# A conformer layer on one core: the convolution's normalization and activation transpose through the convolution's own PSUM banks, and the second sigmoid follows the last rounding

## The chip, the cores and the metric

The kernel runs on one core of one Trainium2 chip. The metric is the device time of one launch in microseconds, the median of several runs. An execution that the hardware profiler recorded gives the span, the rows and the granted TensorE clock quoted here.

## What is computed

One layer on x of 256 rows and 1024 columns, all in fp32:

```
x = x + 0.5 * swiglu(rms_norm(x, g1), w_gate, w_up, w_down)
proj = rms_norm(x, gm) @ w_in
conv_a, conv_b, q, k, v, gate_a, gate_b = split(proj)
u = causal_depthwise_conv(conv_a * sigmoid(conv_b))       # 31 taps
u = silu(layer_norm(u, gain, bias))
y_a = u @ w_conv_proj
y_b = attention(rms_norm(q), rms_norm(k), v) @ w_attn_proj    # 16 heads, causal
x = x + (sigmoid(gate_a) * y_a + sigmoid(gate_b) * y_b) @ w_out
x = x + 0.5 * swiglu(rms_norm(x, g2), w_gate2, w_up2, w_down2)
```

## The kernel before, in words

Every dense product goes through `gemm` (L137). A product of a column chunk of 512 is cut into pieces of two 128-row blocks of the weight; each piece is one transfer of 512 KB from SyncE (SP) into a ring of five `raw` buffers. ScalarE rounds the piece to the matmul type (`hi`, L100), VectorE or GpSimd subtracts (`lo`, L102), both in rings of five, and TensorE runs three matmuls of 512 columns for each block and each half t of the 256 rows (L165 to L167: hi times hi, hi times lo, lo times hi). A transposed activation is split in the same two parts. The results lie in PSUM: a ring `acc` of three banks (L66), a ring `cv` of two banks for the convolution (L69), and a ring `tr` of three banks for transposes and the attention (L72).

The stages follow each other: first feed-forward, input projection `w_in` (14 chunks, in the order of `W_IN`), attention projection `w_attn` (two chunks, `wb`), convolution projection `w_conv` (two chunks, `wa`), output projection `w_out`, second feed-forward. The attention (`score`, `flip`, `value`, L458 to L536) and the convolution are generators that are pumped between the pieces of the input projection and of the first chunk of the attention projection. The written order is only the start: a scheduler that simulates the engines puts the instructions of each engine in order when the program is built, and a ring's bank must have been read before its next user writes it. So which ring an instruction draws from changes where it lands.

What the change touches stands between the attention's end and the convolution projection:

- `conv` (L330) accumulates 31 taps in two `cv` banks on VectorE, and ScalarE copies them back into the tiles `uT` (L350). Four such pairs run one after the other.
- `conv_norm` (L352) transposes `uT` back to rows: for each half t two groups of four transposes (L359) into one PSUM bank each, a ScalarE copy into `ynat` (L364); then VectorE's statistics (L368, L370), `rsqrt_mean` (ScalarE scaling L185, GpSimd power L187), and VectorE's normalization of the half (L375).
- `conv_act` (L378) transposes `ynat` once more, four groups of four transposes (L385), each into one bank; ScalarE applies gain, bias and Silu into `z` (L392, two buffers) and rounds it (`u2h`, L398), VectorE subtracts (`u2l`, L399). `u2h` and `u2l` are what the convolution projection multiplies.
- `run` calls `sigmoid` (L699) on `gate_b` with `issue_after` the attention's last rounding (`oh`, L220), and on `gate_a` with `issue_after` what `conv_act` returns. Sigmoid, Silu and the attention's exponential need different activation tables, so each change of function has a row `ACT_TABLE_LOAD`. `gate_b` is multiplied with the attention projection (L714), `gate_a` with the convolution projection (L722).

Of the kernel before, what the change touches and what calls it, by code (L numbers as in the profile page):

```python
# [50 lines left out]
class Build:  # L51
# [300 lines left out]
    def conv_norm(self, yT, ynat):  # L352
        nc = self.nc
        for t in range(2):
            for c0 in range(0, KD, 4):
                ps = self.tr()
                for q in range(4):
                    c = c0 + q
                    nc.tensor.transpose(  # L359
                        ps[:, q * P : (q + 1) * P],  # L360
                        yT[c // 2][:, (c % 2) * S + t * P : (c % 2) * S + (t + 1) * P],
                        self.ident,
                    )
                nc.scalar.copy(ynat[:, t * D + c0 * P : t * D + (c0 + 4) * P], ps)  # L364
                yield 1
            st = self.tmp.tile([P, 2, 6], F32, tag="bst", name="bst", bufs=2)
            for c in range(2):
                nc.vector.bn_stats(st[:, c, :], ynat[:, t * D + c * CH : t * D + (c + 1) * CH])  # L368
            mv = self.tmp.tile([P, 2], F32, tag="mv", name="mv", bufs=2)
            nc.vector.bn_aggr(mv, st)  # L370
            r = self.rsqrt_mean(mv[:, 1:2], 1, 1)
            yield 1
            for c in range(2):
                y = ynat[:, t * D + c * CH : t * D + (c + 1) * CH]
                nc.vector.tensor_scalar(y, y, mv[:, 0:1], r, ALU.subtract, ALU.mult)  # L375
            yield 1

    def conv_act(self, ynat, hi, lo, after):  # L378
        nc = self.nc
        cst = self.cst  # L380
        for c in range(0, KD, 2):
            ps = self.tr()
            for q in range(2):
                for t in range(2):
                    nc.tensor.transpose(  # L385
                        ps[:, q * S + t * P : q * S + (t + 1) * P],
                        ynat[:, t * D + (c + q) * P : t * D + (c + q + 1) * P], self.ident,
                    )
            z = self.tmp.tile([P, CH], F32, tag="junk", name="z", bufs=2)
            with self.tc.issue_after(after.ins):  # L390
                for q in range(2):
                    last = nc.scalar.activation(  # L392
                        z[:, q * S : (q + 1) * S], ps[:, q * S : (q + 1) * S], AF.Silu,
                        bias=cst[:, C_LB + c + q : C_LB + c + q + 1],
                        scale=cst[:, C_LG + c + q : C_LG + c + q + 1],
                    )
            h = hi[:, c * S : (c + 2) * S]
            nc.scalar.copy(h, z)  # L398
            nc.vector.tensor_tensor(lo[:, c * S : (c + 2) * S], z, h.bitcast(F32), ALU.subtract)  # L399
        return last  # L400


    def head_norm(self, acc, rstd, c, dst, gain, rq=None):
# [437 lines left out]
```

## Time and profile before

| | |
|---|---|
| median of 3 runs | 647.08 us (646.92 to 647.13) |
| profiled execution | 647.48 us, span 645.6 us, mean granted TensorE clock 0.995 |
| TensorE busy | 634.2 us (98%), weight loads 516.8 us |
| VectorE, ScalarE, GpSimd busy | 369.9, 362.5, 164.9 us |
| DMA | 114.97 MB, mean 178 GB/s |

Times in rows are microseconds from the start of the span. A timeline row gives start, duration, engine, line, operation, what is written and read, how many, and in brackets the idle time of the engine before it and what ended it. Matmuls are pipelined, so the rows of neighbours overlap: the distance of two starts is what a matmul costs. The granted clock (PEclk) is a share of full speed; 1.00 is 2.4 GHz and 0.50 is 1.2 GHz.

### The profile page before, as it was taken

Reading aid. Unit: us, or ns where it says so; the run is one execution under the profiler, and the core shown is the slowest. Engines: PE = TensorE matmul, PEld = TensorE weight load, DVE = VectorE, ACT = ScalarE, POOL = GpSimd, SP = SyncE. Lnnn points to the kernel's source line nnn. Section 1 sums busy time; section 2 is a strip of 40 time slices with the busy share of each in tenths; the row PEclk is TensorE's granted clock in tenths of the full one; section 3 lists DMA queues with packets and bytes.
Section 4 is the critical chain, followed back from the end, with each engine's and each line's share of the span. In section 5 each row is a group of like instructions: output and inputs, shape, how many; then the busy total and the mean of one; then the engine's idle time right before and its main releaser. Section 6 shows DMA issues by size and latency. Waiting matters only on the chain.

```text
span 645.6 us, 8133 instructions
## 1 busy us (share of the span) xinstructions
PE 634.2 (98%) x2952; PEld 516.8 (80%) x2952; DVE 369.9 (57%) x625; ACT 362.5 (56%) x547; POOL 164.9 (26%) x83
## 2 busy tenths in 40 slices
PE   9999999999999999999999997899999999999997
PEld 7788888888888888777777785788888888888886
DVE  5655464554542699879313936485664546465541
ACT  6755354443545676987876667744655435444330
POOL 0100000000006999689866761000100000000000
PEclk9999999999999999999999999799999999999999
DMA  8966556567564555545654552264755656556630
GB/s 271 354 232 192 199 173 195 160 198 219 174 201 135 178 170 180 171 130 169 196 158 135 164 168 96 96 199 153 224 163 186 196 177 198 189 168 200 197 124 32
DMA packets 32855, 114.97 MB, mean 178 GB/s; under 512 B 3632, under 2 KB 4912, under 8 KB 32816
## 3 DMA queue, kind: packets, MB, share of 16 engines
q1 hardware_dynamic: 32816, 114.46, 55.9%
q8 instruction: 23, 0.38, 0.2%
q14 instruction: 16, 0.13, 0.1%
HBM read 113.40 MB, written 1.05 MB: 177 GB/s over the span
## 4 chain that ended last, share of the span: by engine, by line
PE 64%; DVE 2%; ACT 1%; issue 0%; DVEq 0%
PE acc L165 20%; PE acc L166 20%; PE acc L167 19%; PE tr L465 1%; PE tr L211 1%; PE tr L529 1%; PE tr L512 1%; DVE lo L102 1%; PE tr L438 1%; DVE bst L368 0%; ACT gate_b L703 0%; ACT z L392 0%; PE tr L655 0%; DVE gate_b L714 0%; ACT L703 0%
## 5 line engine op out<-in xcount | busy, mean ns | idle before, releaser
L100 ACT CAST hi<-raw 128x1024 fp32r<-128x1024 f32 (+1 forms) x216 | 223.1, 1035 | 220.3 <-PE acc L167 184.4
L102 DVE TENSOR_TENSOR lo<-raw,hi 128x1024 fp32r<-128x1024 f32 (+1 forms) x156 | 186.2, 1197 | 167.2 <-ACT hi L100 162.7
L102 POOL TENSOR_TENSOR lo<-raw,hi 128x1024 fp32r<-128x1024 f32 x60 | 143.7, 2420 | 200.3 <-ACT hi L100 200.2
L347 DVE SCALAR_TENSOR_TENSOR cv<-uT,cst,cv 128x255 f32<-128x255 f32 (+28 forms) x240 | 95.2, 465 | 8.4 <-ACT cv L343 8.2
L166 PE MATMUL acc<-lo,h1h 128*128 128x512 f32 x224 | 88.3, 394 | 0.0
L165 PE MATMUL acc<-hi,h1h 128*128 128x512 f32 x224 | 88.0, 398 | 0.2 <-DVE un L646 0.2
L167 PE MATMUL acc<-hi,h1l 128*128 128x512 f32 x224 | 87.3, 393 | 0.0
L165 PE MATMUL acc<-hi,h2h 128*128 128x512 f32 x176 | 69.1, 393 | 0.0
L165 PE MATMUL acc<-hi,aTh 128*128 128x512 f32 x176 | 68.8, 391 | 0.0
L167 PE MATMUL acc<-hi,aTl 128*128 128x512 f32 x176 | 68.5, 389 | 0.0
L166 PE MATMUL acc<-lo,aTh 128*128 128x512 f32 x176 | 68.5, 389 | 0.0
L166 PE MATMUL acc<-lo,h2h 128*128 128x512 f32 x176 | 68.5, 390 | 0.0
L167 PE MATMUL acc<-hi,h2l 128*128 128x512 f32 x176 | 67.2, 390 | 0.0
L166 PE MATMUL acc<-lo,hTh 128*128 128x512 f32 x160 | 62.4, 390 | 0.5 <-DVE lo L102 0.5
L165 PE MATMUL acc<-hi,hTh 128*128 128x512 f32 x160 | 62.2, 392 | 0.0
L167 PE MATMUL acc<-hi,hTl 128*128 128x512 f32 x160 | 62.2, 389 | 0.0
L165 PEld LDWEIGHTS acc<-hi,h1h 128*128 128x128 f32 x224 | 42.1, 188 | 10.3 <-issue 0.7
L167 PEld LDWEIGHTS acc<-hi,h1l 128*128 128x128 f32 x224 | 42.1, 188 | 9.3 <-issue 0.7
L166 PEld LDWEIGHTS acc<-lo,h1h 128*128 128x128 f32 x224 | 42.1, 188 | 8.9 <-issue 0.8
L167 PEld LDWEIGHTS acc<-hi,aTl 128*128 128x128 f32 x176 | 33.0, 188 | 6.9
L165 PEld LDWEIGHTS acc<-hi,aTh 128*128 128x128 f32 x176 | 33.0, 188 | 6.8
L165 PEld LDWEIGHTS acc<-hi,h2h 128*128 128x128 f32 x176 | 33.0, 188 | 6.8
(138 smaller groups left out, 778.8 us busy)
## 6 DMA issues: line engine op xcount, KB each, us to landing
raw<-w_in SPq DMA_DIRECT2D x56, 512.0 KB, 4.2
raw<-w2gu SPq DMA_DIRECT2D x44, 512.0 KB, 4.4
raw<-w1gu SPq DMA_DIRECT2D x40, 512.0 KB, 4.8
raw<-w1d SPq DMA_DIRECT2D x22, 512.0 KB, 4.3
raw<-w2d SPq DMA_DIRECT2D x22, 512.0 KB, 4.4
raw<-w_attn SPq DMA_DIRECT2D x8, 512.0 KB, 4.2
raw<-w_conv SPq DMA_DIRECT2D x8, 512.0 KB, 4.0
raw<-w_out SPq DMA_DIRECT2D x8, 512.0 KB, 4.4
```

The lines of the kernel that those rows point to most:

```text
L100: nc.scalar.copy(hi, raw)
L102: ins = eng.tensor_tensor(lo, raw, hi.bitcast(F32), ALU.subtract)
L165: nc.tensor.matmul(o, ah(k, t), wh, start=st, stop=False)
L166: nc.tensor.matmul(o, ah(k, t), wl, start=False, stop=False)
L167: nc.tensor.matmul(o, al(k, t), wh, start=False, stop=sp)
L211: nc.tensor.transpose(ps[:, q * S + t * P : q * S + (t + 1) * P], src(t, j + q), self.ident)
L347: nc.vector.scalar_tensor_tensor(o, u, w, o, ALU.mult, ALU.add)
L438: nc.tensor.transpose(ps[:, q * S + t * P : q * S + (t + 1) * P], xs[t][:, (j + q) * P : (j + q + 1) * P], self.ident,)
L465: ins = nc.tensor.matmul(ps[q][:, t * P : t * P + (t + 1) * P], qT[r, b * S + t * P : b * S + (t + 1) * P], kT[r, b * S : b * S + (t + 1) ...
L512: nc.tensor.transpose(ps[:, i * P : (i + 1) * P], pr[:, o : o + P], self.ident)
L529: ins = nc.tensor.matmul(ps[q * HD : (q + 1) * HD, kt * P : S], v[:, kt * D + h * HD : kt * D + (h + 1) * HD], pT[:, o : o + n], start=kt ...
```

## The change

Two edits. `conv_norm` and `conv_act` take their PSUM bank from the `cv` ring of two banks and no longer from the `tr` ring of three. And `conv_act` returns the last rounding (L398) in place of the last Silu (L392), so the second sigmoid is issued after that rounding.

```
         for t in range(2):
             for c0 in range(0, KD, 4):
-                ps = self.tr()
+                ps = self.cv()
...
         for c in range(0, KD, 2):
-            ps = self.tr()
+            ps = self.cv()
...
                 for q in range(2):
-                    last = nc.scalar.activation(
+                    nc.scalar.activation(
                         z[:, q * S : (q + 1) * S], ps[:, q * S : (q + 1) * S], AF.Silu,
...
-            nc.scalar.copy(h, z)
+            rounded = nc.scalar.copy(h, z)
             nc.vector.tensor_tensor(lo[:, c * S : (c + 2) * S], z, h.bitcast(F32), ALU.subtract)
-        return last
+        return rounded
```

What it does to the order is best seen on three pieces; a number behind a name tells one buffer from another. On TensorE, in the first piece of the attention projection's second chunk (`acc_3585`), the transposes back to rows (L359) now stand between its matmuls:

```order
 L166 MATMUL acc_3585<-lo_3589,oh_1543 128x512 [waits Pool_49]
+L359 MATMUL cv_3316<-ident_91,uT0_1535 128x128 [waits Activation_49]
+L359 MATMUL cv_3316<-ident_91,uT0_1535 128x128
+L359 MATMUL cv_3316<-ident_91,uT1_1536 128x128 x2
 L167 MATMUL acc_3585<-hi_3588,ol_1544 128x512
 L165 MATMUL acc_3585<-hi_3588,oh_1543 128x512
 L166 MATMUL acc_3585<-lo_3589,oh_1543 128x512
+L359 MATMUL cv_3322<-ident_91,uT2_1537 128x128 [waits Activation_49]
+L359 MATMUL cv_3322<-ident_91,uT2_1537 128x128
+L359 MATMUL cv_3322<-ident_91,uT3_1538 128x128 x2
 L167 MATMUL acc_3585<-hi_3588,ol_1544 128x512
```

Before, these eight stood behind the last value product of the attention (L529 into `tr_3257`), some forty rows further on. The other eight (second half) now follow the last flips (L512); before, they stood behind the first eight.

On ScalarE, from the attention's next to last rounding to the first sigmoid, the copies and the scaling of the statistics now come first:

```order
+L364 COPY ynat_1539<-cv_3316 128x512 [waits PE_49]
+L364 COPY ynat_1539<-cv_3322 128x512 [waits PE_49]
 L220 CAST oh_1543<-tr_3185 128x256 [waits PE_49]
 L515 COPY pT_3218<-tr_3219 128x384 [waits PE_49]
+L185 ACTIVATE ms_3333<-mv_3331 128x1 [waits DVE_49]
 L515 COPY pT_3218<-tr_3224 128x384 [waits PE_49]
+L364 COPY ynat_1539<-cv_3357 128x512 [waits PE_49]
+L364 COPY ynat_1539<-cv_3363 128x512 [waits PE_49]
+L185 ACTIVATE ms_3374<-mv_3372 128x1 [waits DVE_49]
 L220 CAST oh_1543<-tr_3257 128x256 [waits PE_49]
 L703 ACT_TABLE_LOAD
 L703 ACTIVATE gate_b_3077<-gate_b_3077 128x512 x4
```

Before, the four copies and both scalings stood behind the four sigmoids of `gate_b`, the scalings between casts of the convolution projection's weights. On VectorE the statistics and both normalizations now stand before the first gate product (L714) in the same way.

On TensorE ahead of the convolution projection (`acc_3663`), with the change, the third and fourth group of the activation's transposes:

```order
L167 MATMUL acc_3586<-hi_3642,ol_1544 128x512
L385 MATMUL cv_3561<-ident_91,ynat_1539 128x128 [waits PE_49,Activation_49]
L385 MATMUL cv_3561<-ident_91,ynat_1539 128x128 x3
L385 MATMUL cv_3571<-ident_91,ynat_1539 128x128 [waits PE_49,Activation_49]
L385 MATMUL cv_3571<-ident_91,ynat_1539 128x128 x3
L165 MATMUL acc_3663<-hi_3666,u2h_3459 128x512 [waits DVE_49,Activation_49]
```

Before, all four groups stood here:

```order
L385 MATMUL tr_3541<-ident_91,ynat_1539 128x128 [waits DVE_49,Activation_49]
L385 MATMUL tr_3551<-ident_91,ynat_1539 128x128 [waits Activation_49]
L385 MATMUL tr_3561<-ident_91,ynat_1539 128x128 [waits DVE_49,Activation_49]
L385 MATMUL tr_3541<-ident_91,ynat_1539 128x128 [waits DVE_49]
L385 MATMUL tr_3541<-ident_91,ynat_1539 128x128 x2
L385 MATMUL tr_3551<-ident_91,ynat_1539 128x128 x3
L385 MATMUL tr_3561<-ident_91,ynat_1539 128x128 [waits DVE_49]
L385 MATMUL tr_3561<-ident_91,ynat_1539 128x128 x2
L385 MATMUL tr_3571<-ident_91,ynat_1539 128x128 [waits PE_49,Activation_49]
L385 MATMUL tr_3571<-ident_91,ynat_1539 128x128 x3
L165 MATMUL acc_3663<-hi_3666,u2h_3459 128x512 [waits Activation_49]
```

With the change the first and second group (`cv_3541`, `cv_3551`) stand earlier, the last six of their transposes right ahead of the 24 matmuls of `acc_3586`, so that these 24 lie between the second and the third group. On ScalarE the table load and the four sigmoids of `gate_a`, before between the last Silu and the last two roundings, now stand behind the last rounding, with one weight cast between the two roundings. The instructions of SP and GpSimd are the same in the same order.

## Rows read from the trace of the kernel before

**Rows 1.** Windows: length, busy PE, PEld, DVE, ACT, POOL; PEclk, DMA share, GB/s

```profile
380.40:391.70 11.30, 11.30 (x67) 8.70 (x66) 0.85 (x2) 5.47 (x10) 4.74 (x2) 1.00 0.44 139
399.80:405.20 5.40, 1.09 (x6) 0.36 (x4) 5.40 (x9) 2.58 (x4) 2.17 (x2) 0.87 0.89 303
405.20:410.80 5.60, 5.30 (x19) 4.25 (x20) 1.68 (x3) 4.37 (x10) 0.00 (x0) 0.52 0.44 146
410.80:640.00 229.20, 229.20 (x1050) 190.02 (x1049) 123.43 (x131) 107.07 (x131) 1.64 (x1) 1.00 0.54 168
```

**Rows 2.** Timeline of TensorE (PE), 380 to 411

```profile
380.60 0.39 PE L166 MATMUL acc<-lo,oh 128*128 128x512 f32 x1
...
388.59 1.09 PE L359 MATMUL tr<-ident,uT 128*128 128x128 f32 x8
389.44 0.48 PE L166 MATMUL acc<-lo,oh 128*128 128x512 f32 x1
...
391.73 0.95 PE L167 MATMUL acc<-hi,ol 128*128 128x512 f32 x3
...
394.43 0.50 PE L165 MATMUL acc<-hi,oh 128*128 128x512 f32 x1 [0.66 <-DVE gate_b L714]
...
399.78 0.39 PE L167 MATMUL acc<-hi,ol 128*128 128x512 f32 x1
401.50 0.76 PE L385 MATMUL tr<-ident,ynat 128*128 128x128 f32 x3 [1.33 <-ACT ms L185]
405.18 3.13 PE L385 MATMUL tr<-ident,ynat 128*128 128x128 f32 x13 [2.93 <-DVE ynat L375]
408.62 0.80 PE L165 MATMUL acc<-hi,u2h 128*128 128x512 f32 x1 [0.30 <-ACT u2h L398]
...
410.76 0.39 PE L166 MATMUL acc<-lo,u2h 128*128 128x512 f32 x1
```

**Rows 3.** Timeline of ScalarE (ACT), 377 to 412

```profile
377.55 0.37 ACT L350 COPY uT<-cv 128x256 f32<-128x256 f32 x1
...
379.57 2.10 ACT L100 CAST hi<-raw 128x1024 fp32r<-128x1024 f32 x2
...
388.71 0.37 ACT L220 CAST oh<-tr 128x256 fp32r<-128x256 f32 x1 [4.41 <-PE tr L529]
389.10 1.28 ACT L703 ACT_TABLE_LOAD   x1
390.39 2.19 ACT L703 ACTIVATE gate_b<-gate_b 128x512 f32<-128x512 f32 x4
392.49 1.54 ACT L364 COPY ynat<-tr 128x512 f32<-128x512 f32 x3
...
406.12 1.93 ACT L392 ACTIVATE z<-tr,cst 128x256 f32<-128x256 f32 x4 [3.43 <-PE tr L385]
...
411.34 1.28 ACT L703 ACT_TABLE_LOAD   x1
```

**Rows 4.** Timelines of VectorE (DVE) and GpSimd (POOL), 380 to 406

```profile
393.09 0.69 DVE L368 BATCH_NORM_STATS2 bst<-ynat 128x6 f32<-128x512 f32 x1 [3.55 <-ACT ynat L364]
...
404.59 1.00 DVE L375 TENSOR_SCALAR ynat<-ynat,mv,rs 128x512 f32<-128x512 f32 x2
...
380.70 4.74 POOL L102 TENSOR_TENSOR lo<-raw,hi 128x1024 fp32r<-128x1024 f32 x2 [0.58 <-ACT hi L100]
398.76 1.34 POOL L187 TENSOR_TENSOR rs<-ms,neghalf 128x1 f32<-128x1 f32 x1 [13.32 <-ACT ms L185]
401.48 1.88 POOL L187 TENSOR_TENSOR rs<-ms,neghalf 128x1 f32<-128x1 f32 x1 [1.38 <-ACT ms L185]
```

**Rows 5.** The page: VectorE's weight subtractions; loads of w_out (last: us to landing)

```profile
L102 DVE TENSOR_TENSOR lo<-raw,hi 128x1024 fp32r<-128x1024 f32 (+1 forms) x156 | 186.2, 1197 | 167.2 <-ACT hi L100 162.7
...
raw<-w_out SPq DMA_DIRECT2D x8, 512.0 KB, 4.4
```

**Rows 6.** Timeline of SyncE's DMA queue (SPq), 360 to 440

```profile
402.97 28.61 SPq L151 DMA_DIRECT2D raw<-w_out  x8
```

## The prediction

> **What bounds the kernel now.** The page's busy times (the table above) put TensorE far ahead of all others, so I looked for where it is not busy. The view by stretches tells: TensorE is busy without a gap at full granted clock from 380.4 to 391.7 and again from 410.8 to 640 [rows 1]. Between these lies the only weak place: in 399.8 to 405.2 it is busy 1.09 of 5.40 us, and in 405.2 to 410.8 its granted clock is 0.52, that is the lower level of 1.2 GHz [rows 1]. What it waited for stands in its timeline: 0.66 us for the gate product (L714), 1.33 us for the second statistics (L185), 2.93 us for the normalized rows (L375), 0.30 us for the rounded activation (L398) [rows 2].
>
> Price of the weak place. From 391.73 to 410.76 TensorE issues 32 matmuls of 512 columns (3 at 391.73, 24 from 394.43 on, 5 from 408.62 on) and 20 transposes (4 L359, 16 L385). A matmul takes (399.78 - 394.43)/23 = 0.23 us when nothing waits, a transpose (389.44 - 388.59)/8 = 0.106 us [rows 2]. That is 32 x 0.23 + 20 x 0.106 = 9.5 us of work in 19.0 us: **9.5 us are lost there**, part waiting, part at half clock. Since TensorE is full on both sides, whatever of this is saved comes off the end.
>
> Why it is lost: the normalization is late. Its first transposes start at 388.59 [rows 2], behind the last attention value product; its copies on ScalarE at 392.49, behind the attention's last rounding (388.71), a table load (389.10) and four sigmoids (390.39) [rows 3]; statistics on VectorE from 393.09, with gate products and weight subtractions (1.2 us each) between them [rows 4, 5]; the second half is normalized from 404.59 on [rows 4]. Yet the convolution left its two banks long before: the last copy out of them starts at 377.55 and takes 0.37 us [rows 3]. So between 377.9 and 388.6 these banks stand empty.
>
> **The change, part by part.** No instruction is added or removed; SP and POOL issue the same instructions in the same order. Three things move.
>
> *Transposes of the convolution (L359).* Sixteen move ahead on TensorE: two groups of four into the piece that in the trace follows the L166 at 380.60 [rows 2], two groups behind the last flips. They need only the last convolution copy (377.92 [rows 3]): no wait. Cost on TensorE: the same 16, but in more separate runs; I set 0.2 us for that, below zero being excluded because work is the same, and 0.6 us above (the 0.66 gap is the nearest price of one interruption [rows 2]).
>
> *Copies, statistics, normalization.* ScalarE takes the first two copies right behind the two weight casts that end at 379.57 + 2.10 = 381.7 [rows 3]; a copy costs 1.54/3 = 0.51 us [rows 3]. The second group of transposes ends near 382.4, its copy near 383.0; two statistics at 0.69 us each [rows 4] end about 384, aggregate and scaling about 384.9. POOL is in order and busy with weight subtractions until 380.70 + 4.74 = 385.4 [rows 4]; then the power, 1.34 to 1.88 us [rows 4]: 386.8 to 387.3. Normalizing takes 1.0 us [rows 4]: 388. The second half repeats: its copies end near 387, its statistics wait for the first normalization on VectorE's queue, 389.2; power at about 391; normalized at **391.9 to 392.4**. In the trace of before they end at 404.59 + 1.00 = 405.6 [rows 4]. TensorE's own order wants these rows just ahead of 24 attention-projection matmuls and two more transposed groups. The place of the first convolution-projection matmul with nothing lost before it: 408.62 - (408.62 - 391.73 - 27 x 0.23 - 20 x 0.106) = 400.1. Going back 8 transposes, 24 matmuls and 6 transposes, the rows are wanted at 400.1 - 0.85 - 5.5 - 0.6 = 393.1. Slack about 1 us: the waits of 1.33 and 2.93 us go.
>
> Queued behind the new early waits: on ScalarE the second scaling (L185) now stands ahead of the attention's last rounding. It is done about 389.4, the rounding 0.37 us later [rows 3], at 389.8; TensorE wants it nine matmuls ahead of 393.1, at 391.0. Covered, by 1.2 us. The table load and sigmoids then run 389.8 to 393.2 (1.28 + 2.1 us [rows 3]); the first gate product, wanted to free a bank at 393.7, needs only the first sigmoid (391.7) and lies near 393.2. Covered by half a microsecond: the thinnest cover, and what is late next if anything is.
>
> *Activation and second sigmoid.* ScalarE: one weight cast of 1.05 us to 394.2, table load to 395.5, four Silu 1.93 us to 397.4 [rows 3], rounding (as a copy of that size) to 398.0. TensorE wants the bank of the first Silu at 400.1 - 0.85 = 399.2 and the rounded rows at 400.1: two microseconds of cover, so the 0.30 us wait goes, and the 24 matmuls are now what fills the time. Next: three casts and four Silu end near 404.6, their rounding 405.2; wanted 25 matmuls after 400.1, at 405.9. Cover 0.7 us. The second sigmoid, which in the trace of before started at 411.34 between those Silu and their rounding [rows 3], now stands behind both roundings and one cast: 406.8 to 410.2. Behind it come a cast (411.3) and its subtraction on VectorE (1.2 us [rows 5]: 412.5) for weights that TensorE wants 61 matmuls after 400.1, at 414.1. I cost that at nothing, the cover being 1.6 us; without it the move would cost up to its own 3.4 us.
>
> The weight transfers keep their order on SP and are released by VectorE's subtractions, which come at nearly the same times as before, while TensorE wants the weights 8.5 us earlier. The first output-projection load starts at 402.97 and such a load takes 4.4 us [rows 5, 6]: in at 408, cast and wanted only near 423. Behind, the DMA share is 0.54 [rows 1]. So I cost them at nothing; a wait there would be bounded by one load's 4.4 us.
>
> *Sum.* 9.5 us lost before, minus 0.2 us of interruptions, and with TensorE never idle its clock stays at the upper level: **gain 9.3 us**. The profiled execution took 647.48 us (span 645.6), 0.4 above the median of 647.08. Against it the sum gives 638.2, against the median 637.8.
>
> What the table load costs is read from the rows: the rounding ends at 388.71 + 0.37 = 389.08, the load runs 389.10 to 390.38, the first sigmoid starts 390.39 [rows 3]; nothing stands around it, so I take 1.28 us a switch and keep twice that as the upper bound (fourth rival). The Trainium skill ("ScalarE: Activation LUTs", section "What ACT_TABLE_LOAD costs") gives a switch a drain of 1.38 us beside a load of 1.28, which by the covers above would make the gain 2.1 us smaller (an estimate); the trace agrees with the load and shows no drain.
>
> **The rivals.**
>
> 1. *The statistics chain stays as slow as it was.* From the first copy to the end of the second normalization it took 404.59 + 1.00 - 392.49 = 13.1 us [rows 3, 4]. Started at 381.7 it would end at 394.8 in place of 392.4: 394.8 - 393.1 = 1.7 us of wait, and half a microsecond more for the bank behind. Time 637.8 + 2.2 = 640.0. For it: every engine is in order. Against: VectorE's queue holds no gate product or subtraction between these steps now.
>
> 2. *Two banks are too few.* The third transposed group of the activation must wait until the Silu has read the first; before, a third bank was there. If ScalarE is 4 us later than worked out, its second pair of Silu ends at 401.4, the fourth group is wanted at 399.6, TensorE waits 2 us there and the clock falls as in 405.2 to 410.8 [rows 1]: 8 x 0.106 + 5 x 0.23 = 2.0 us more. Time 637.8 + 4.0 = 641.8. The Trainium skill has a rule on this side ("TensorE: Matmul & The Clock Gate", section "A second HAM failure mode: psum-queue depth-cycling"): pauses between groups of matmuls that cycle through PSUM banks bring the clock down. The rows agree that the clock falls when TensorE pauses, after the waits of 1.33 and 2.93 us [rows 1, 2]. Against it here: 24 matmuls lie between the second and the third group.
>
> 3. *Slower: ScalarE's queue holds up the attention.* The last rounding waits behind the second scaling, and the nine matmuls behind it stop, with everything after. Each microsecond that the scaling comes later than 390.6 is one of time; it decides against the kernel from 9.3 us on, so with a chain of 390.6 + 9.3 - 381.7 = 18 us from the first copy to the second scaling. Before, even the whole chain to the end of normalizing took 13.1 us. At 20 us the time would be 637.8 + 11.1 = 648.9. Against it: nothing in these queues takes so long.
>
> 4. *A table switch costs more in this order*, at most its own row again, 1.28 us. Two lie on the way to the Silu: 2.6 us later, against covers of 2 us at the first rounding and 0.7 at the third, so 1.9 us of waiting in all, time 639.7. The rows around the load speak against it.
>
> 5. *The change doesn't free anything*, because a wait by order keeps the transposes behind the attention: 647.1. The order of instructions speaks against it.
>
> **How the numbers follow.** Forecast 72%, rival 1 13%, rival 2 4%, rival 3 3%, rival 4 5%, rival 5 3%. The predicted time is the forecast's, 637.8. Low end: all of the 9.5 us saved is 637.6, and the loss, a sum over 52 rounded durations, may be half a microsecond larger, 637.0. High end: rivals 1 and 4 and a missed cover of half a microsecond beyond, 640.6. Left out above are rivals 2, 3 and 5, 10%, and some of the tails. Faster by more than 0.2% (1.3 us, about what a measurement of this kernel can tell from no change): 95%, all but rivals 3 and 5, with a little of the others. Within it 2%, slower 3%.
>
> **What would show it.** Right: no wait over 0.5 us on TensorE between 380 and 412, a granted clock of 1.00 throughout, the first ynat copy on ScalarE near 382, the normalized second half near 392, the first convolution-projection matmul near 400, the second table load for the sigmoid behind both roundings. Rival 1 shows as a wait of the second normalized transposes for L375; rival 2 as a wait for the Silu before the third group with clock 0.5; rival 3 as a wait for L220. A gap in the output projection with casts waiting for transfers would show that the loads do not keep up, and that I have mispriced them.

## The result, and the profile after

| | before | after |
|---|---|---|
| median (4 runs each, same chip) | 647.11 us (646.92 to 647.91) | **638.44 us** (637.88 to 639.63) |
| ratio | | 0.9866, 95% interval 0.9848 to 0.9884 |
| profiled execution | 647.48, span 645.6 | 638.96, span 637.1 |
| mean granted TensorE clock | 0.995 | 1.000 |

The change makes the kernel 8.7 us faster; forecast were 9.3, and 637.8 us. In the table of the experiments below, one of the four runs of the kernel N took 1640.67 us, a thousand more than the other three, and is left out of its median. The loss stood in one place, so that place is read first. TensorE's waits in the whole execution after (line waited for; us in total, times, longest):

```profile
PE tr L574 <- DVE idle L571: 1.1, 1, 1.1
PE acc L166 <- DVE lo L102: 0.5, 1, 0.5
PE cv L132 <- ACT hi L100: 0.2, 1, 0.2
PE acc L165 <- DVE un L646: 0.2, 1, 0.2
```

Three lie in the first 20 us, and the last (L646) at 209, far ahead of the place. The waits of 0.66, 1.33, 2.93 and 0.30 us [rows 2] have no successor. The windows after, at the same times as in [rows 1]:

```profile
380.40:391.70 11.30, 11.30 (x70) 8.66 (x69) 5.35 (x12) 7.04 (x14) 6.33 (x5) 1.00 0.44 139
...
399.80:405.20 5.40, 5.40 (x29) 4.55 (x28) 5.25 (x6) 5.40 (x10) 0.00 (x0) 1.00 0.46 127
405.20:410.80 5.60, 5.60 (x26) 4.65 (x25) 3.01 (x4) 5.57 (x9) 0.00 (x0) 1.00 0.89 313
410.80:632.00 221.20, 221.20 (x1015) 183.45 (x1014) 120.99 (x129) 100.75 (x121) 1.63 (x1) 1.00 0.55 172
```

In the two middle windows TensorE was busy 1.09 and 5.30 us at 0.87 and 0.52 of its clock before; now it is full at 1.00. VectorE's work in the window from 380.4 rose from 0.85 to 5.35 us: the statistics have moved there, under the attention. The timeline of TensorE after shows the new order:

```profile
381.42 0.39 PE L166 MATMUL acc<-lo,oh 128*128 128x512 f32 x1
381.64 0.60 PE L359 MATMUL cv<-ident,uT 128*128 128x128 f32 x4
...
386.47 1.03 PE L359 MATMUL cv<-ident,uT 128*128 128x128 f32 x8
...
394.08 0.82 PE L385 MATMUL cv<-ident,ynat 128*128 128x128 f32 x6
394.66 0.48 PE L165 MATMUL acc<-hi,oh 128*128 128x512 f32 x1
...
400.22 1.04 PE L385 MATMUL cv<-ident,ynat 128*128 128x128 f32 x8
401.02 0.48 PE L165 MATMUL acc<-hi,u2h 128*128 128x512 f32 x1
...
402.26 0.39 PE L166 MATMUL acc<-lo,u2h 128*128 128x512 f32 x1
```

The first row is the matmul that stood at 380.60 before, the last one the sixth of the convolution projection, at 410.76 before [rows 2]. Between them lay 30.16 us and lie 20.84 now: **9.32 us gained in the place**. Behind it nothing changed: from that sixth matmul to the last matmul of the kernel it was 230.57 us and is 230.52.

This execution gained 8.5 us over the profiled one before, and not 9.3, because it reached the place 0.8 us later: the matmul ahead of it starts at 381.42, not at 380.60. That comes from the first 20 us, where TensorE waits for the first weights by different amounts in different runs (0.24 us for the first L100 here, none before; in another run of the same kernel 0.42 and 0.91): the matmul that waits for L102 starts at 17.60 before and at 18.37 here. That the medians gained 8.7 for the same reason is likely but not shown, since only one run of each kernel has rows. To be free of this I measure every kernel below also by **the stretch**: from the value product L529 near 367, the last one ahead of anything the edits move, to the start of the last matmul. TensorE before:

```profile
367.14 0.87 PE L529 MATMUL tr<-pT,v 128*64 128x256 f32 x8
...
641.33 0.39 PE L167 MATMUL acc<-hi,aTl 128*128 128x512 f32 x1
```

That is 274.19 us. After, the two start at 367.96 and 632.78: 264.82 us, 9.37 less. In the traces of all kernels used here that value product starts between 367.04 and 368.47, in changed and unchanged ones alike.

ScalarE after, the rows of the steps that the prediction put times to:

```profile
382.38 0.58 ACT L364 COPY ynat<-cv 128x512 f32<-128x512 f32 x1
...
389.29 0.20 ACT L185 ACTIVATE ms<-mv 128x1 f32<-128x1 f32 x1 [1.11 <-DVE mv L370]
390.40 0.37 ACT L220 CAST oh<-tr 128x256 fp32r<-128x256 f32 x1 [0.91 <-PE tr L529]
390.79 1.28 ACT L703 ACT_TABLE_LOAD   x1
392.09 2.19 ACT L703 ACTIVATE gate_b<-gate_b 128x512 f32<-128x512 f32 x4
...
398.34 0.63 ACT L398 CAST u2h<-z 128x512 fp32r<-128x512 f32 x1
...
404.98 0.64 ACT L398 CAST u2h<-z 128x512 fp32r<-128x512 f32 x1
...
406.44 0.65 ACT L398 CAST u2h<-z 128x512 fp32r<-128x512 f32 x1
407.10 1.28 ACT L703 ACT_TABLE_LOAD   x1
```

VectorE after, around the second normalization and the first gate products:

```profile
390.81 0.42 DVE L221 TENSOR_TENSOR ol<-tr,oh 128x256 fp32r<-128x256 f32 x1 [1.55 <-ACT oh L220]
391.15 0.99 DVE L375 TENSOR_SCALAR ynat<-ynat,mv,rs 128x512 f32<-128x512 f32 x2
393.90 1.89 DVE L714 TENSOR_TENSOR gate_b<-acc,gate_b 128x512 f32<-128x512 f32 x3 [1.75 <-PE acc L167]
```

GpSimd after, the two powers:

```profile
386.19 0.56 POOL L187 TENSOR_TENSOR rs<-ms,neghalf 128x1 f32<-128x1 f32 x1
389.57 0.55 POOL L187 TENSOR_TENSOR rs<-ms,neghalf 128x1 f32<-128x1 f32 x1 [2.82 <-ACT ms L185]
```

The first copy starts at 382.38 in place of 392.49 [rows 3], and the second half is normalized at 392.14 in place of 405.59 [rows 4]. The second table load for the sigmoid stands behind all four roundings.

### The profile page after: what moved, and what is told of

Its sections match the earlier page's. It is cut to its first block, busy times and chain, and to the rows that moved or that the text cites. A ratio compares the mean times of both kernels' runs of the same rounds, so it can differ in the third digit from the quotient of the medians.

```text
span 637.1 us, 8135 instructions
## 1 busy us (share of the span) xinstructions
PE 631.2 (99%) x2952; PEld 515.8 (81%) x2952; DVE 370.4 (58%) x625; ACT 362.0 (57%) x547; POOL 162.7 (26%) x83
## 3 DMA queue, kind: packets, MB, share of 16 engines
HBM read 113.40 MB, written 1.05 MB: 180 GB/s over the span
## 4 chain that ended last, share of the span: by engine, by line
PE 67%; DVE 0%; DVEq 0%; issue 0%
PE acc L165 20%; PE acc L166 20%; PE acc L167 20%; PE tr L465 1%; PE tr L211 1%; PE tr L529 1%; PE tr L512 1%; PE tr L438 1%; PE tr L655 0%; PE cv L385 0%; PE cv L359 0%; DVE un L646 0%; DVE ot L754 0%; DVEq L830 0%
## 5 line engine op out<-in xcount | busy, mean ns | idle before, releaser
L100 ACT CAST hi<-raw 128x1024 fp32r<-128x1024 f32 (+1 forms) x216 | 222.8, 1035 | 215.8 <-PE acc L167 182.1
L102 DVE TENSOR_TENSOR lo<-raw,hi 128x1024 fp32r<-128x1024 f32 (+1 forms) x156 | 186.2, 1196 | 168.7 <-ACT hi L100 164.0
L102 POOL TENSOR_TENSOR lo<-raw,hi 128x1024 fp32r<-128x1024 f32 x60 | 143.6, 2415 | 200.9 <-ACT hi L100 200.8
L167 PE MATMUL acc<-hi,h1l 128*128 128x512 f32 x224 | 87.4, 393 | 0.0
L167 PE MATMUL acc<-hi,aTl 128*128 128x512 f32 x176 | 68.5, 389 | 0.0
L167 PE MATMUL acc<-hi,h2l 128*128 128x512 f32 x176 | 67.2, 390 | 0.0
L167 PE MATMUL acc<-hi,hTl 128*128 128x512 f32 x160 | 62.2, 390 | 0.0
L167 PEld LDWEIGHTS acc<-hi,h1l 128*128 128x128 f32 x224 | 42.1, 188 | 9.3 <-issue 0.7
L167 PEld LDWEIGHTS acc<-hi,aTl 128*128 128x128 f32 x176 | 33.0, 188 | 6.9
L166 PEld LDWEIGHTS acc<-lo,aTh 128*128 128x128 f32 x176 | 33.1, 188 | 6.8
```

Of the source, the lines that this page charges most:

```text
L100: nc.scalar.copy(hi, raw)
L102: ins = eng.tensor_tensor(lo, raw, hi.bitcast(F32), ALU.subtract)
L166: nc.tensor.matmul(o, ah(k, t), wl, start=False, stop=False)
L167: nc.tensor.matmul(o, al(k, t), wh, start=False, stop=sp)
```

## The experiments

Three edits can be made alone: **N**, the normalization's bank from `cv`; **A**, the activation's bank from `cv`; **S**, the sigmoid behind the rounding. My theory: N carries all, S is needed beside A at most. The rivals: the two parts need each other, or S is what frees the path.

| kernel | median us | ratio to before, 95% | stretch us |
|---|---|---|---|
| before | 647.1 to 647.7 by chip | | 274.19 |
| after (N, A, S) | 638.44 | 0.9866 (0.9848 to 0.9884) | 264.82 |
| after, again | 639.08 | 0.9875 (0.9860 to 0.9889) | 264.80 |
| N | 639.14 | 0.9870 (0.9854 to 0.9887) | 265.16 |
| A | 648.27 | 1.0011 (1.0001 to 1.0020) | 274.54 |
| S | 647.65 | 1.0000 (0.9991 to 1.0009) | 274.52 |
| N, S | 638.42 | 0.9862 (0.9847 to 0.9877) | 264.80 |
| N, A | 640.19 | 0.9882 (0.9865 to 0.9898) | 266.46 |
| half of N, A, S | 646.77 | 0.9982 (0.9973 to 0.9992) | 273.14 |
| before, one wait filled | 646.32 | 0.9980 (0.9970 to 0.9989) | 272.93 |
| after, ScalarE delayed by 4 copies | 644.53 | 0.9950 (0.9935 to 0.9964) | 271.24 |
| after, ScalarE delayed by 2 copies | 639.19 | 0.9877 (0.9860 to 0.9893) | 265.60 |
| after, VectorE kept busy | 642.22 (one run) | | 268.77 |

Each stretch is that of one execution. S, whose waits in the place are those of before, is 0.33 us longer because two more matmuls behind the waits ran at the lower clock (the fifth and sixth of the convolution projection), so a third of a microsecond means little in kernels whose clock falls.

**N alone.** Before, with

```
@@ conv_norm
-                ps = self.tr()
+                ps = self.cv()
```

> Only the first bank line: the normalization's transposes (L359) draw from the convolution's two banks, the activation's from the old ring of three, the second sigmoid stays behind the last Silu. Theory A (the gain comes from starting the normalization before the attention ends): nearly all of the gain is here, 638.4 to 639.5 us. One weak spot: the last rounding now stands behind table load, sigmoids and a cast, up to 1 us of wait there. Theory B (the gain needs the activation's banks and the sigmoid's place as well, each worth some microseconds): 641 to 645 us.

It gains 647.64 - 639.14 = 8.5 us, nearly as much as the whole change. The same kernel once more (one run, 638.79 us), for its profile:

> The kernel of e1 once more, for its rows (the profiled execution of e1 was disturbed by a millisecond): the 0.8 us that e1 lies above the whole change should stand in TensorE's waits as one wait for the last rounding (L398) or the weights cast behind the sigmoids, of 0.5 to 1.2 us, with the granted clock at 1.00. If not, the 0.8 us lies elsewhere.

The wait that was expected isn't there: no wait of the place is left in its list. Its stretch is 265.16, 0.34 us above that of the whole change. Most of the 0.34 is one pause: the second sigmoid there stands ahead of the fourth rounding (table load at 404.23, rounding at 408.56), and the two matmuls at 408.83 take 0.73 us in place of 0.46 to the next start.

**A alone.** The same line in `conv_act`.

> Only the second bank line: the activation's transposes (L385) draw from the convolution's two banks, everything else as before. Theory A: no change, 646.8 to 647.5 us; the place of all instructions is as before, and the third group now has to wait for the first Silu where it had a third bank, hidden behind the same wait. Theory B: 643 to 645 us.

Nothing is gained; the second normalization is as late as before, and the waits for it (1.24 and 3.34 us) are about as long as the two before (1.33 and 2.93 us). The third group isn't wholly hidden: the last eight transposes wait 0.47 us more for a Silu to read their banks. The median, 648.27, lies above the expected range, but on this chip the kernel before took 647.64 and not 647.1.

**S alone.** `conv_act` returns `rounded`.

> Only the return value: the second sigmoid behind the last rounding, banks as before. Theory A: no change, 646.8 to 647.5 us, since TensorE is busy from 410.8 on with either order. Theory B: 645 to 646.5 us.

Ratio 1.0000 (647.65 against 647.64 on the same chip): in the order of before the second sigmoid isn't on the path at all.

**N and S.**

> The normalization on the convolution's banks and the second sigmoid behind the last rounding, the activation on the old ring of three. Theory A: as good as the whole change, 637.9 to 638.7 us, without a wait of the last rounding. Theory B (two banks in the activation matter): 640 us or more, or, if two banks cost something, below 637.5 us.

Median and stretch equal those of the whole change (638.42 and 638.44, 264.80 and 264.82). A is worth nothing once N and S are there.

**N and A.** What S does for it:

> Both bank lines, the second sigmoid as before behind the last Silu. Theory A: as the whole change or up to 0.7 us above, 637.9 to 639.2 us; the third and fourth rounding come 3.4 us later (table load and four sigmoids), against a cover that the trace of the changed kernel puts at 1.2 us at the third, but the scheduler sets six matmuls of the next chunk ahead (1.4 us). Theory B (the sigmoid's place is worth some microseconds by itself): 640 us or more.

A miss: 640.19 is above the 639.2 that theory A allowed, and the stretch is 1.64 us longer than after, where it allowed 0.7. The cover and the six matmuls together were too little. One new wait, of TensorE:

```profile
409.58 0.50 PE L165 MATMUL acc<-hi,u2h 128*128 128x512 f32 x1 [1.10 <-ACT u2h L398]
```

and ScalarE of the same kernel tells why:

```profile
405.54 1.28 ACT L703 ACT_TABLE_LOAD   x1
406.83 2.19 ACT L703 ACTIVATE gate_a<-gate_a 128x512 f32<-128x512 f32 x4
408.93 0.60 ACT L398 CAST u2h<-z 128x512 fp32r<-128x512 f32 x1
```

The third rounding stands behind the sigmoid's load and its four rows, 3.4 us, which without S use up the cover and 1.1 us more. The granted clock stays at its upper level (length, busy PE, PEld, DVE, ACT, POOL; PEclk, DMA share, GB/s):

```profile
408.00:413.00 5.00, 3.90 (x18) 2.91 (x17) 3.18 (x4) 4.32 (x7) 0.00 (x0) 1.00 0.53 166
```

So S mainly repairs what A, for the scheduler, puts in that order. Beside N alone it takes 0.36 us off the stretch, and alone it gains nothing. A and S without N were not run.

**Half of the normalization in the old ring.** To make the statistics late without adding work:

```
@@ conv_norm, the change
-                ps = self.cv()
+                ps = self.cv() if t == 0 else self.tr()
```

> The whole change, but the second half (t = 1) of the normalization's transposes draws from the old ring, so it lands behind the attention again. Theory A: the second half's statistics set the end; reckoned through the queues its normalization ends near 401 where TensorE wants it at 400, and the first rounding is near 404: three to four microseconds come back and the clock falls for a while: 641 to 644 us. If halving gave half, 642.7. Theory B (what matters is that the old ring is relieved, by half here): 638.5 to 640 us.

A miss: 646.77, nearly all of the gain is gone. TensorE:

```profile
395.71 0.61 PE L165 MATMUL acc<-hi,oh 128*128 128x512 f32 x1 [2.01 <-DVE gate_b L714]
...
399.46 0.40 PE L165 MATMUL acc<-hi,oh 128*128 128x512 f32 x1
...
403.77 0.87 PE L385 MATMUL cv<-ident,ynat 128*128 128x128 f32 x6 [0.69 <-DVE ynat L375]
406.60 2.03 PE L385 MATMUL cv<-ident,ynat 128*128 128x128 f32 x8 [1.95 <-ACT z L392]
```

The window at its last transposes (length, busy PE, PEclk, DMA share, GB/s):

```profile
406.00:409.00 3.00, 2.40 (x10) 0.53 0.70 228
```

I had counted the late normalization, but not what it takes with it. VectorE's first gate product stood behind a statistics instruction that waited for the late copy (2.01 us), and the nine matmuls behind that wait took 3.75 us to 399.46, where 0.23 each makes 2.1. The last eight transposes found both banks unread (1.95 us) and then ran at half clock, 2.03 us where such a row takes 1.04 after. Of the 8.32 us by which the stretch is longer than after, 4.65 are listed waits, and most of the rest is the lower clock behind them. The wait for the banks is the second rival's mechanism. A alone has a short one too (0.47 us), but there the clock was down before it.

**A filled wait.** How much of the 9.5 us is clock, and how much waiting? Before, with 24 transposes whose result nobody reads, of the half that was ready:

```
@@ conv_act, before
             ps = self.tr()
+            if c == 4:
+                for r in range(24):
+                    nc.tensor.transpose(ps[:, :P], ynat[:, r % 8 * P : (r % 8 + 1) * P], self.ident)
```

> The kernel before, with 24 transposes of the already normalized half, results thrown away, ahead of the third transposed group, so that TensorE works in the wait of 2.93 us. They take 24 x 0.106 = 2.5 us inside that wait. If the lower clock behind the wait cost as much as the rows say (5 matmuls 1.0 us, and the transposes on the way to the first Silu some 0.3 to 0.7 us), the clock stays up and the time falls to 645.3 to 646.0 us. If the clock's part is hidden by other waits: 646.8 to 647.5 us. If the repeated transposes stretch the wait: above 647.5 us.

The windows of this kernel (length, busy PE, PEclk, DMA share, GB/s):

```profile
399.80:405.20 5.40, 4.07 (x32) 1.00 0.85 266
405.20:410.80 5.60, 3.83 (x22) 1.00 0.57 205
```

The median, 646.32, falls between the first two ranges; against the kernel before on the same chip (647.69) it is 1.37 us faster. The clock stays at 1.00, its upper level, and the stretch shortens by 274.19 - 272.93 = 1.26 us. The data is just as late: the second half is normalized 38.4 us behind the value product near 367 in both kernels. So holding the clock up is worth 1.3 us; the other 8 are waiting, which goes when the data comes earlier.

**How wide is the cover of the first rounding?** A cover is the time by which a result is ready before TensorE wants it. After, with 512-column copies behind the first sigmoid, on ScalarE:

```
@@ run, the change
         last = sigmoid(gb, self.last_att)
+        pad = self.const.tile([P, CH], F32, name="pad")
+        with tc.issue_after(last.ins):
+            for i in range(4):
+                last = nc.scalar.activation(pad, gb[:, 3 * CH :], AF.Copy)
```

> The changed kernel with four copies of 512 columns on ScalarE behind the first sigmoids (1.9 us), results thrown away; the scheduler then also sets two casts ahead of the first rounding (1.9 us). In the trace of the changed kernel the first rounding ends at 399.0 and TensorE wants it at 401.0. With 3.8 us more it ends at 402.7: a wait of 1.6 to 1.8 us, no fall of the clock, time 640.0 to 640.4 us against 638.4. If the covers are larger than I read: 638.4. If the pause brings the clock down: 641 us or more.

A miss: 644.53, on a chip where the kernel before took 647.69, so 3.2 us of gain are left where some 7 were expected. The delay came as expected: with the copies and the two weight casts (2.00 us) the first rounding starts at 402.17 in place of 398.34, and TensorE's wait for it is 1.74 us. Not expected were a second wait, of 0.93 us, for a subtraction (L399) that stood on VectorE behind two weight subtractions and a gate product, and the fall of the clock. TensorE's timeline, the rows that waited, and the first at the upper clock again:

```profile
400.46 0.66 PE L385 MATMUL cv<-ident,ynat 128*128 128x128 f32 x4 [0.19 <-ACT z L392]
402.86 0.50 PE L165 MATMUL acc<-hi,u2h 128*128 128x512 f32 x1 [1.74 <-ACT u2h L398]
404.99 0.79 PE L167 MATMUL acc<-hi,u2l 128*128 128x512 f32 x1 [0.93 <-DVE u2l L399]
...
410.70 0.46 PE L167 MATMUL acc<-hi,u2l 128*128 128x512 f32 x1
```

The windows of this kernel (length, busy PE, PEclk, DMA share, GB/s):

```profile
403.00:406.00 3.00, 2.07 (x6) 0.67 0.69 197
406.00:409.00 3.00, 3.00 (x9) 0.50 0.76 224
409.00:412.00 3.00, 3.00 (x11) 0.69 0.77 281
```

The waits add up to 2.86 us, the stretch is longer by 271.24 - 264.82 = 6.42. The rest is mostly clock: the 13 matmuls from 404.99 on took 5.71 us to 410.70, where 0.23 each makes 3.0, so 2.7 us went there. By the windows, in which the clock was on average short of its upper level by 0.33, 0.50 and 0.31, in 3 us each, it was at most 3.4.

With two copies, `range(2)`:

> The changed kernel with two copies of 512 columns on ScalarE behind the first sigmoids (0.9 us), results thrown away; one cast of 0.95 us also comes ahead of the first rounding by the scheduler's order. The first rounding then ends near 400.7 where TensorE wants it at 401.0. Theory A (a cover of 2 us, a threshold, nothing lost below it): 638.2 to 638.8 us, at most one wait, under 0.4 us. Rival (every delay on ScalarE costs in proportion, the 1.9 us kernel having cost 6 us): about 641 us.

The median, 639.19, is within 0.2 us of the change's repeat (639.08) and above the range of theory A. The stretch is 0.78 us longer than after, where theory A allowed 0.4, in two pauses of 0.3 us and smaller ones that the list of waits doesn't show. ScalarE there has 1.30 us of copies and again a cast (1.05 us) ahead of the first rounding, 2.3 us later in all. So the cover of that rounding is just used up: some 2 us, as predicted. The rival's 641 did not come.

**VectorE busy beside the power.** After, with three subtractions of 512 columns beside each power on GpSimd, whose result nobody reads (`pad` is a tile made for them):

```
@@ conv_norm, the change
             r = self.rsqrt_mean(mv[:, 1:2], 1, 1)
+            for c in range(3):
+                nc.vector.tensor_tensor(
+                    self.pad, ynat[:, t * D : t * D + CH], ynat[:, t * D + CH : (t + 1) * D], ALU.subtract
+                )
```

> The changed kernel with three subtractions of 512 columns on VectorE beside each of the two powers on GpSimd (L187), results thrown away. The power took 1.34 and 1.88 us in the kernel before, with VectorE at work beside it, and 0.56 and 0.55 us in the changed one, with VectorE idle. If VectorE's work is the cause: 1.2 to 1.9 us for a power that has a subtraction beside it; if it is the place in the program: 0.55 us. The second normalization comes 2 to 4 us later against a cover of 1.9 us, so the time may be 638 to 642 us.

GpSimd of this kernel:

```profile
380.87 4.73 POOL L102 TENSOR_TENSOR lo<-raw,hi 128x1024 fp32r<-128x1024 f32 x2 [0.57 <-ACT hi L100]
386.58 0.98 POOL L187 TENSOR_TENSOR rs<-ms,neghalf 128x1 f32<-128x1 f32 x1 [0.98 <-ACT ms L185]
393.81 0.56 POOL L187 TENSOR_TENSOR rs<-ms,neghalf 128x1 f32<-128x1 f32 x1 [6.25 <-ACT ms L185]
```

VectorE of the same kernel, the added subtractions in the run of the first weight subtraction, of the first power, and with GpSimd idle:

```profile
384.01 2.14 DVE L373 TENSOR_TENSOR pad<-ynat 128x512 f32<-128x512 f32 x1
...
386.48 1.40 DVE L373 TENSOR_TENSOR pad<-ynat 128x512 f32<-128x512 f32 x2
...
390.10 0.68 DVE L373 TENSOR_TENSOR pad<-ynat 128x512 f32<-128x512 f32 x1
```

The power takes 0.98 us with a subtraction beside it, and 0.55 to 0.56 without; the 1.2 us or more that I expected wasn't reached. Only the first power had a subtraction beside it. The scheduler set the second scaling behind the four sigmoids, at 393.54, when the added subtractions were done, and it moved six transposes of normalized rows, which stand ahead of the 24 matmuls in the changed kernel (394.08), behind 20 of them (398.67). So the time of this kernel, 642.22, is not the price of a busy VectorE alone. A row of TensorE's timeline, and a window over its longest wait (length, busy PE, PEld, DVE, ACT, POOL; PEclk, DMA share, GB/s):

```profile
394.00 0.50 PE L165 MATMUL acc<-hi,oh 128*128 128x512 f32 x1 [0.40 <-DVE gate_b L719]
```

```profile
400.00:406.00 6.00, 3.47 (x18) 2.23 (x17) 4.01 (x5) 5.07 (x9) 0.00 (x0) 1.00 0.88 294
```

TensorE's waits here (0.40 for the gate product, 1.48 and 0.26 for Silu, 0.80 for the rounding) add up to 2.94 us, the stretch is longer by 3.95 us, and the clock stays at 1.00. Counted from the starts of the matmuls, these four pauses come to 3.7 us, so they are nearly all of it.

**The change again**, on the chip of the kernels with two copies and with VectorE busy:

> The changed kernel again, on the same chip as the delayed one, as its yardstick: 637.9 to 639.6 us as before, gain 8.5 to 9.3 us. The runs of one kernel differ by up to 1.7 us; if this comes from the first loads, the rows of the first 20 us differ and those from 20 us on do not.

Gain 647.16 - 639.08 = 8.1 us, below the 8.5 expected at least; stretch 264.80, and its waits beyond those of the first profile all lie in the first 20 us. By the stretch the two executions agree within 0.02 us; the medians, 0.6 apart, don't.

## Why the prediction was right

- **The loss and the sum**: 9.5 us of loss less 0.2 of interruptions is 9.3; the place gained 9.32, the stretch 9.37. Right. The median moved by 8.7, 0.6 less than forecast; the profiled executions differ by 0.8 in the first 20 us. 638.44 lies in the range.
- **The mechanism**: transposes that need only empty banks move ahead, the statistics run under the attention. Right, and N alone shows it. What I left open is how the gain splits over the parts: A gives nothing, S nothing alone.
- **The statistics chain**: predicted 391.9 to 392.4, measured 392.14, wanted by TensorE at 394.08 (predicted 393.1). The time is right by errors that cancel. The power took 0.55 us, not the 1.34 to 1.88 of [rows 4], so the second one was done at 390.12. But the normalization stood on VectorE behind the attention's last subtraction (L221), which waited for the last rounding until 390.81; that queue I had not followed. And all of this execution is 0.8 us later. From the first copy to the end of the second normalization it took 9.8 us, not the 13.1 of the first rival.
- **The last attention rounding**: predicted to wait for the second scaling. It waited for TensorE's value product (L529) and not for ScalarE; the third rival's wait never showed.
- **The first gate product**: named as the thinnest cover, half a microsecond. The first of the three rows from 393.90 ends near 394.55, TensorE goes on at 394.66: 0.1 us. It did not wait for the sigmoid, as predicted, but 1.75 us for TensorE's own last matmuls of that bank (L167), and the six transposes from 394.08 fill the time that it takes. In the kernel with VectorE busy these six stand elsewhere, and TensorE waits 0.40 us; with the late half it cost 2.01.
- **The first rounding**: predicted cover 2 us; it ends at 398.97, TensorE starts the convolution projection at 401.02. Right, and the two delays agree.
- **The third rounding and the second sigmoid**: predicted 405.2, measured 405.62, no wait. Without S it came at 409.5 and cost 1.10 us.
- **A table switch** at its own row: the rounding ends at 390.77, the load starts at 390.79 and the first sigmoid at 392.09. The drain of 1.38 us that the Trainium skill names ("ScalarE: Activation LUTs", section "What ACT_TABLE_LOAD costs") has no room in these 0.02 us. The fourth rival has no support.
- **Loads**: those of `w_out` start at 404.67 and no cast waits in a way that reaches TensorE. Costed at nothing, rightly.
- **The second rival** is a real mechanism in a wrong place: in this kernel nothing triggers it, but a late half of the normalization does (1.95 us of waiting for Silu, then half clock).

## What to carry to other kernels

A buffer ring is also an order: when a scheduler or a program order waits for banks, a chain that could start early starts late because it draws from a ring that a later stage holds, so look for the ring that is already empty. Cost a dependent chain up to the instruction that is wanted, and for each in-order queue on the way ask what else stands behind the late one: with half of the chain late, the gate product, the banks and the lower clock behind their waits took back nearly all of the gain. A cover is a threshold: against a cover of 2 us, a delay of 2.3 us cost 0.8 here, and one near 4 us cost 6.4, because a second wait came with it and the clock fell.

## What the runs showed of the hardware

- *The same waits cost differently.* Waits of 2.9 us in all cost 3.95 us where the granted clock stayed at 1.00 (VectorE kept busy) and 6.42 us where it fell to 0.50 (ScalarE delayed). A single wait of 1.10 us (N and A) left it at 1.00. Which pauses bring it down I didn't try to settle.
- *GpSimd and VectorE slow each other.* The power on 128 elements takes 0.55 us with VectorE idle, 0.98 beside VectorE's subtractions, and was 1.34 to 1.88 before, beside its weight subtractions [rows 4]; a VectorE subtraction of 512 columns takes 0.68 us alone and 2.14 beside GpSimd's weight subtractions. The Trainium skill ("SBUF — State Buffer", section "Who interferes with whom") says that a VectorE instruction with two inputs in SBUF contends with a GpSimd instruction that reads SBUF; both rows agree. That the slower powers made the chain of 13.1 us before any longer is not shown: each was done (at 400.10 and 403.36) before VectorE's queue came to the normalization (400.86 and 404.59).
